# Two hybrid decoder layers on one core: first query tile's items one projection later, its causal mask in the bias table, and the norms' constant on VectorE

## Chip, cores and metric

The kernel runs on one core of one Trainium2 chip. The metric is the time of one execution on the device, in microseconds. Before the change the median of three runs was 1549.06 us (1547.16 to 1550.01).

## The reference

Two decoder layers run over 512 tokens of width 1024. Each layer has a token mixer, a cross attention into 256 memory tokens and a SwiGLU feed-forward network, and behind each of the three stands a layer norm over the residual:

```python
x = layer_norm(ALPHA * x + mixer(x), ln_g[i, 0], ln_b[i, 0])
x = layer_norm(ALPHA * x + cross_attention(x, mem), ln_g[i, 1], ln_b[i, 1])
x = layer_norm(ALPHA * x + swiglu_ffn(x), ln_g[i, 2], ln_b[i, 2])
# layer_norm: (x - mean) * rsqrt(var + 1e-5) * g + b
```

Layer 0 mixes with latent attention (MLA, 16 heads), whose two compressed inputs pass an RMS norm first. Layer 1 mixes with a sparse attention (DSA, 16 heads in 4 groups). A small indexer gives a score to each pair of query and key; for each query the 128 best keys among the earlier ones are kept; the attention logits of the kept keys get a bias, which depends on the distance between query and key and on the head, and all other keys count for nothing:

```python
score = where(causal, sum_h(w_idx * relu(q_idx @ k_idx.T)), -inf)
sel = top_k(score, 128)
logits = q @ k[sel].T * 64 ** -0.5 + rel_bias[t5_bucket(pos_q - pos_k[sel])]
out = softmax(where(sel <= q_index, logits, -inf)) @ v[sel]
```

## The kernel before

**Arithmetic.** A matrix product in f32 is done as three products of rounded parts. Each operand is split into a rounded value (an ACT cast, L98) and the rest (a subtraction, L100, on VectorE (DVE) or GpSimd (POOL)), and TensorE (PE) runs high times high, high times low and low times high (L121 to L123, `mm3`). One projection of 512 tokens onto 128 columns is 24 matmuls of 128x512.

**Stages.** The program has no loop on the device; the Python loops write everything out. Layer 0 is the MLA mixer with its RMS norms (`rms_t`, L508 to L522, eight of them, two for each of four token tiles), then its output projection with the layer norm, the cross attention with its own, and FFN 0 with its own. Then comes layer 1 in the same manner, with the DSA mixer, and the last norm writes the result. The order of each engine's instructions is set by a scheduler from the program's text; the waits between engines are semaphores.

**Layer norm.** `Norm.stat` (L298) takes statistics of a half row of a token tile (L300). `Norm.finish` (L302) joins them (L304) and calls `rstd_of` (L268): on POOL a multiply-add with the constant (L270) and a power of -0.5 (L272). Then, for each half, DVE subtracts the mean and multiplies by the gain (L323), and multiplies by the result of the power and adds the offset (L325); PE transposes the tile (L329) and the transposed tile is split. The last norm of the kernel (L307 to L320) has another form: the two subtractions (L309), then a first piece on DVE (L314), a second one on ACT and POOL (L317, L318), and the write to the output (L319). `LASTS` (L285) sets where these pieces are cut: at column 512, and at 704 in the last token tile. `out_proj` (L345) calls the norm. Its last part runs over the four token tiles; in the last one of the kernel the product is done in two column halves (`TAIL`), each with residual (L341) and statistics, and `finish` of the tile before stands ahead of the first residual (L378). `rms_t` uses `rstd_of` too: an ACT square with a sum, the constant and the power on POOL, then DVE's product with the result (L514).

**DSA mixer.** The value projection, the indexer's projections and its scores come first (L912 to L950). For query tiles 1 to 3 the scores lie in `masks[qt]`, 256, 384 and 512 columns wide. `topk` (L959) does one round: MAX8 (L964) finds the eight largest of a row, MATCH_REPLACE8 (L965) strikes them out. Sixteen rounds make 128 keys, and behind the last one a TENSOR_SCALAR (L969) turns the struck-out places into a mask of 0 and -BIG (2 to the 100th). The 48 rounds of the three tiles are handed out: two ahead of each of two key projections, and five (`NTK`) ahead of each of eight query projections (L1087 to L1101) until none is left. The mask of query tile 0 is plain causality and is written at the start: a POOL memset and select into `mk0f`, and a DVE cast (L956).

Each query projection gives two heads. `stack_q_pool` (L902) splits them: three ACT copies and two POOL subtractions (L907, L908), so that the two parts lie stacked and the scores need two matmuls instead of three. An item is a query tile with a group of four heads, 16 in all, and has three words: `s` (scores, `dsa_scores`, L1003), `t` (transposes, `dsa_t`, L1017) and `p` (times the values, `dsa_pv`, L1034). For each head, `s` runs a product of the identity and the mask (L1011), which puts the mask into the PSUM bank, and two products of Q and K (L1012, L1013); then DVE adds the bias and finds the row's extreme (L410, in `Softmax.exp`) and ACT does the exponential (L416). The table `steps` (L1079) says which words stand behind which query projection, and what follows the loop is written out (L1103 on):

```python
steps = {1: "s0", 2: "t0", 3: "s1 p0", 4: "t1", 5: "s2 p1", 6: "t2", 7: "s3 p2"}
```

Items 0 to 3 are query tile 0. Item 3 needs heads 12 to 15, that is, projections 6 and 7; item 0 needs projections 0 and 1.

**Bias table.** `bias_table` (L246), written ahead of all that and running far earlier, makes the row of biases by distance with a product of the 16 heads' table and a 0/1 matrix `onehot` of 640 (`GW`) columns, in two column blocks, 0 to 512 and 512 to 640. The last 128 columns stand for keys behind the query. The table is spread over a DRAM scratch, from which each item reads its window. `general_bias` (L181) is a branch that runs only where the positions aren't consecutive.

## Time and profile before

| | |
|---|---|
| runs, median (range) | 1549.06 us (1547.16 to 1550.01) |
| the profiled execution | 1549.22 us |
| its span, first to last instruction | 1547.4 us |
| mean granted clock of PE | 0.998 |
| PE busy | 1509.4 us, 98% |
| DVE busy | 997.8 us, 64% |
| ACT busy | 649.9 us, 42% |
| POOL busy | 321.6 us, 21% |
| DRAM read and written | 161.20 and 9.47 MB |

In a row of the timeline the columns are the start in us, the duration in us, the engine, the line, the operation, output and inputs with their sizes, how many instructions the row holds, and in brackets the idle time of the engine just before with the instruction that ended it. In a row of groups the count is followed by the busy time in us and the mean of one in ns, and then by the idle time before them. In a row of waits the idle time of the first engine is followed by how often it occurred and the longest one. In the table of stretches each engine has its busy time and the number of its instructions; the granted clock, the share of the DMA engines and the transfer rate follow. PEld is the loading of weights into PE, which overlaps the matmuls. An engine's idle time costs only where the engine, or someone who waits for it, sets the end.

### The profile page before, as it was taken

The numbers are of one execution on the slowest core, as the hardware profiler recorded it, in microseconds if no ns is written. First come the engines' busy times: TensorE is split into PE (matmuls) and PEld (weight loads), VectorE is DVE, ScalarE is ACT, GpSimd is POOL, SyncE is SP. The second block draws the span as 40 slices with busy tenths as digits, with TensorE's granted clock in tenths as the row PEclk, the third lists the DMA queues.
The fourth block names the chain that finished last, engine by engine and source line by source line (L and its number), as shares of the span: only waits on it lengthen the run. The fifth ranks groups of instructions, "written<-read, shape, count | busy, mean of one in ns | idle before, by whom it ended". The sixth has DMA issues, their size and how long they took to land.

```text
span 1547.4 us, 20800 instructions
## 1 busy us (share of the span) xinstructions
PE 1509.4 (98%) x7940; PEld 1287.3 (83%) x7940; DVE 997.8 (64%) x1709; ACT 649.9 (42%) x1150; POOL 321.6 (21%) x332
## 2 busy tenths in 40 slices
PE   9999999999999999999999899999999999999997
PEld 8788888988888888888887688898988888888886
DVE  6887868454746565654668989675548465656545
ACT  4677743343233333332246568334432333333230
POOL 1322001000132331400124553010002323324003
PEclk9999999999999999999999999999999999999999
DMA  6234424322323232223242147333323232322221
GB/s 221 71 102 116 138 82 133 126 83 95 125 94 109 77 118 92 96 95 109 83 143 96 35 140 255 109 109 110 107 89 132 73 118 88 106 96 93 96 95 55
DMA packets 51320, 166.79 MB, mean 108 GB/s; under 512 B 5300, under 2 KB 11748, under 8 KB 49172
## 3 DMA queue, kind: packets, MB, share of 16 engines
q1 hardware_dynamic: 50788, 164.41, 31.6%
q8 instruction: 62, 1.02, 0.3%
q10 hardware_dynamic: 432, 1.05, 0.2%
q14 instruction: 38, 0.31, 0.1%
HBM read 161.20 MB, written 9.47 MB: 110 GB/s over the span
## 4 chain that ended last, share of the span: by engine, by line
PE 83%; DVE 7%; ACT 3%; POOL 3%; issue 2%; DMA 2%; POOLq 0%; ACTq 0%; DVEq 0%; SPq 0%
PE ps L121 26%; PE ps L123 26%; PE ps L122 26%; DVE t L100 2%; ACT wh L98 1%; DVE wl L100 1%; ACT t L98 1%; PE ps L1028 1%; ACT t L416 1%; PE ps L329 1%; POOL sm L272 1%; DVE t L325 1%; DMA raw<-in_xa_q_dram 1%; POOL sm L270 1%; PE ps L624 1%
## 5 line engine op out<-in xcount | busy, mean ns | idle before, releaser
L121 PE MATMUL ps<-t,wh 128*128 128x512 f32 (+1 forms) x1264 | 459.7, 364 | 3.4 <-DVE t L100 3.4
L122 PE MATMUL ps<-t,wh 128*128 128x512 f32 (+1 forms) x1264 | 458.2, 363 | 1.6 <-DVE t L100 1.6
L123 PE MATMUL ps<-t,wl 128*128 128x512 f32 (+1 forms) x1264 | 458.2, 362 | 0.0
L98 ACT CAST wh<-raw 128x1024 fp32r<-128x1024 f32 (+2 forms) x218 | 227.3, 1044 | 456.3 <-PE ps L122 173.6
L100 DVE TENSOR_TENSOR wl<-raw,wh 128x1024 fp32r<-128x1024 f32 (+2 forms) x197 | 253.8, 1290 | 226.5 <-ACT wh L98 224.8
L121 PE MATMUL ps<-wh,t 128*128 128x512 f32 (+2 forms) x838 | 305.1, 364 | 2.8 <-DVE t L100 1.5
L123 PE MATMUL ps<-wh,t 128*128 128x512 f32 (+2 forms) x838 | 303.1, 362 | 0.0
L122 PE MATMUL ps<-wl,t 128*128 128x512 f32 (+2 forms) x838 | 302.5, 361 | 0.0
L121 PEld LDWEIGHTS ps<-t,wh 128*128 128x128 f32 x1264 | 238.6, 189 | 41.4 <-DVE t L100 5.5
L122 PEld LDWEIGHTS ps<-t,wh 128*128 128x128 f32 x1264 | 238.7, 189 | 38.0 <-DVE t L100 2.0
L123 PEld LDWEIGHTS ps<-t,wl 128*128 128x128 f32 x1264 | 238.6, 189 | 37.1
L121 PEld LDWEIGHTS ps<-wh,t 128*128 128x128 f32 x838 | 159.2, 190 | 26.4 <-DVE t L100 1.7
L123 PEld LDWEIGHTS ps<-wh,t 128*128 128x128 f32 x838 | 159.0, 190 | 23.9 <-DVE t L100 0.3
L122 PEld LDWEIGHTS ps<-wl,t 128*128 128x128 f32 x838 | 159.2, 190 | 23.0
L98 ACT CAST t<-ps 128x512 fp32r<-128x512 f32 (+2 forms) x249 | 122.7, 526 | 132.0 <-PE ps L329 87.4
L270 POOL TENSOR_SCALAR sm<-sm 128x1 f32<-128x1 f32 x32 | 18.9, 590 | 675.7 <-DVE sm L304 634.7
L100 DVE TENSOR_TENSOR t<-ps,t 128x512 fp32r<-128x512 f32 (+2 forms) x249 | 144.1, 606 | 21.6 <-ACT t L98 20.7
L98 ACT CAST wh<-t 128x1024 fp32r<-128x1024 f32 x56 | 58.9, 1052 | 141.6 <-PE ps L122 123.6
L100 DVE TENSOR_TENSOR wl<-t,wh 128x1024 fp32r<-128x1024 f32 x56 | 71.2, 1272 | 64.9 <-ACT wh L98 63.1
L843 DVE TENSOR_TENSOR t<-ps,t 128x512 f32<-128x512 f32 x44 | 30.4, 692 | 120.4 <-PE ps L123 120.4
L100 DVE TENSOR_TENSOR t<-t,t 128x512 fp32r<-128x512 f32 (+2 forms) x113 | 83.9, 746 | 23.6 <-ACT t L98 21.4
L98 ACT CAST t<-t 128x512 fp32r<-128x512 f32 (+2 forms) x113 | 64.4, 574 | 57.9 <-POOL t L777 33.6
(177 smaller groups left out, 1684.1 us busy)
## 6 DMA issues: line engine op xcount, KB each, us to landing
raw<-in_ffn_in_dram SPq DMA_DIRECT2D x88, 512.0 KB, 3.2
t<-in_ffn_dg_dram SPq DMA_DIRECT2D x16, 1024.0 KB, 5.1
raw<-in_xa_k_dram SPq DMA_DIRECT2D x16, 512.0 KB, 3.3
raw<-in_xa_v_dram SPq DMA_DIRECT2D x16, 512.0 KB, 3.7
raw<-in_xa_q_dram SPq DMA_DIRECT2D x16, 512.0 KB, 3.7
raw<-in_xa_o_dram SPq DMA_DIRECT2D x16, 512.0 KB, 3.3
raw<-in_ffn_dl_dram SPq DMA_DIRECT2D x12, 512.0 KB, 3.2
scr<-vscr SPq DMA_DIRECT2D x16, 319.5 KB, 4.2
```

Source lines behind the costliest of these rows:

```text
L98: nc.scalar.copy(h, src)
L100: (eng or nc.vector).tensor_tensor(l, src, h.bitcast(F32), op=ALU.subtract)
L121: nc.tensor.matmul(ps, st[0], mv[0], start=start, stop=False, skip_group_check=more)
L122: nc.tensor.matmul(ps, st[0], mv[1], start=False, stop=False, skip_group_check=more)
L123: nc.tensor.matmul(ps, st[1], mv[0], start=False, stop=stop, skip_group_check=more)
L270: nc.gpsimd.tensor_scalar(a, var, scale, eps, op0=ALU.mult, op1=ALU.add)
L272: nc.gpsimd.tensor_tensor(b, a, mhalf, op=ALU.pow)
L325: nc.vector.scalar_tensor_tensor(x_of(tt)[:, sl], x_of(tt)[:, sl], rs, self.gb[:, 1, sl], op0=ALU.mult, op1=ALU.add)
L329: nc.tensor.transpose(pt[:, k], x_of(tt)[:, 512 * n + P * k:512 * n + P * k + P], ident)
L416: nc.scalar.activation(Sx, src, AF.Exp, bias=nb, scale=scale, accum_out=self.sm[:, i:i + 1])
L624: nc.tensor.transpose(pt[:, P * qt:P * qt + P], Ss[qt][:, P * kb:P * kb + P], ident)
L843: nc.vector.tensor_tensor(sg, pu, sg, op=ALU.mult)
```

## The change

Four things change. The words of items 0 to 3 in `steps` each move one projection later, and s3 and p2 stand directly behind the loop. The mask of query tile 0 goes: `mk0f`, its cast and its entry in `masks` are gone, the product L1011 is only run for tiles 1 to 3, and the last 128 columns of the bias table hold -BIG in place of a bias (a POOL memset and a DMA; the second column block of the product with `onehot` is gone). The branch for other positions gets a select in the diagonal block instead. In `rstd_of` the constant is added on DVE instead of POOL; the power stays on POOL. In the last norm the last tile is cut at 768 instead of 704, and `finish` of the tile before stands behind the first half's residual and statistics instead of ahead of them.

```diff
--- before.py
+++ after.py
@@ -239,6 +239,9 @@
                             if b:
                                 g.tensor_tensor(acc[c], acc[c], tmp, op=ALU.add)
                     for c in range(4):
+                        if kb == qt:
+                            g.affine_select(out=acc[c], in_=acc[c], pattern=[[0, 4], [-1, P]], compare_op=ALU.is_ge,
+                                            fill=-BIG, base=0, channel_multiplier=1)
                         g.dma_start(scr[1 + qt, 4 * c:4 * c + 4, :, c0 + P * kb:c0 + P * kb + P].rearrange("h p k -> p h k"),
                                     acc[c])
         yield
@@ -247,17 +250,16 @@
 
         relb = t2()
         nc.sync.dma_start(relb[0:32, 0:16], A["rel_bias"])
-        cols = ((0, 512), (512, GW))
-        ohs = [t2() for _ in cols]
-        for oh, (lo, hi) in zip(ohs, cols):
-            nc.sync.dma_start(oh[0:32, 0:hi - lo], A["onehot"][:, lo:hi])
+        oh = t2()
+        nc.sync.dma_start(oh[0:32], A["onehot"][:, 0:S])
         yield
-        for oh, (lo, hi) in zip(ohs, cols):
-            pb = bank("a")
-            nc.tensor.matmul(pb[0:16, 0:hi - lo], relb[0:32, 0:16], oh[0:32, 0:hi - lo], start=True, stop=True)
-            vb = t2()
-            nc.scalar.mul(vb[0:16, 0:hi - lo], pb[0:16, 0:hi - lo], 8.0)
-            nc.sync.dma_start(vscr[:, lo:hi], vb[0:16, 0:hi - lo])
+        pb = bank("a")
+        nc.tensor.matmul(pb[0:16], relb[0:32, 0:16], oh[0:32], start=True, stop=True)
+        vb, vn = t2(), t2(F32, (P, GW - S))
+        nc.scalar.mul(vb[0:16], pb[0:16], 8.0)
+        nc.sync.dma_start(vscr[:, 0:S], vb[0:16])
+        nc.gpsimd.memset(vn[0:16], -BIG)
+        nc.sync.dma_start(vscr[:, S:GW], vn[0:16])
         yield
 
     def bias_rows(h):
@@ -267,7 +269,7 @@
 
     def rstd_of(var, scale, eps):
         a = small()
-        nc.gpsimd.tensor_scalar(a, var, scale, eps, op0=ALU.mult, op1=ALU.add)
+        nc.vector.tensor_scalar(a, var, scale, eps, op0=ALU.mult, op1=ALU.add)
         b = small()
         nc.gpsimd.tensor_tensor(b, a, mhalf, op=ALU.pow)
         return b
@@ -282,7 +284,7 @@
         nc.sync.dma_start(gb[:, 1], A["ln_b"][i, j:j + 1].broadcast_to((P, D)))
         return gb
 
-    LASTS = (((0, 512), (512, 1024)), ((0, 704), (704, 1024)))
+    LASTS = (((0, 512), (512, 1024)), ((0, 768), (768, 1024)))
     TAIL = ((0, 256), (256, 512))
 
     class Norm:
@@ -374,10 +376,13 @@
                             sh, sl = src(k)
                             wh, wl = ws[k // 2]
                             mm3(p1[:, c0:c1], (sh[:, ts_], sl[:, ts_]), (wh[:, k % 2, c0:c1], wl[:, k % 2, c0:c1]), k == 0, k == nk - 1)
-                        if tt and c0 == 0:
+                        early = len(parts) > 1
+                        if tt and c0 == 0 and not early:
                             norm.finish(tt - 1)
                         residual(p1, tt, n, first, c0, c1)
                         norm.stat(tt, n, c0, c1)
+                        if c0 == 0 and early:
+                            norm.finish(tt - 1)
                 norm.finish(NT - 1)
 
     HALVES = ((0, 256), (256, 512))
@@ -948,13 +953,7 @@
             if j == 3:
                 nc.gpsimd.affine_select(out=acc[:, n - P:n], in_=acc[:, n - P:n], pattern=[[-1, P]],
                                         compare_op=ALU.is_ge, fill=-1e30, base=0, channel_multiplier=1)
-    mk0f = t2()
-    nc.gpsimd.memset(mk0f[:, 0:256], 0.0)
-    nc.gpsimd.affine_select(out=mk0f[:, 0:256], in_=mk0f[:, 0:256], pattern=[[-1, 256]],
-                            compare_op=ALU.is_ge, fill=-BIG, base=0, channel_multiplier=1)
     MK = t8()
-    nc.vector.tensor_copy(MK[:, 0, 0:256], mk0f[:, 0:256])
-    masks[0] = MK[:, 0]
 
     def topk(qt, its):
         n = P * (qt + 1)
@@ -1008,8 +1007,9 @@
         sx = Softmax([bt[:, i, 0:n] for i in range(4)])
         for i in range(4):
             ps = bank("b")
-            nc.tensor.matmul(ps[:, :N], identr, masks[qt][:, :N], start=True, stop=False)
-            nc.tensor.matmul(ps[:, :N], Q[4 * g + i][:, ts_], KA[g][:, :N], start=False, stop=False)
+            if qt:
+                nc.tensor.matmul(ps[:, :N], identr, masks[qt][:, :N], start=True, stop=False)
+            nc.tensor.matmul(ps[:, :N], Q[4 * g + i][:, ts_], KA[g][:, :N], start=qt == 0, stop=False)
             nc.tensor.matmul(ps[:, :N], Q[4 * g + i][:, ts_], KB[g][:, :N], start=False, stop=True)
             sx.exp(i, ps[:, :n], 0.125, bt[:, i, 0:n])
         return sx
@@ -1076,7 +1076,7 @@
         PT[i] = dsa_t(*items[i], Ss.pop(i))
 
 
-    steps = {1: "s0", 2: "t0", 3: "s1 p0", 4: "t1", 5: "s2 p1", 6: "t2", 7: "s3 p2"}
+    steps = {2: "s0", 3: "t0", 4: "s1 p0", 5: "t1", 6: "s2 p1", 7: "t2"}
 
     def run(word):
         kind, i = word[0], int(word[1:])
@@ -1100,6 +1100,8 @@
         for word in steps.get(j, "").split():
             run(word)
 
+    run_s(3)
+    run("p2")
     run_s(4)
     run_t(3)
     for i in range(3, 16):
```

What this does to the order of the engines' instructions is shown at three places. Line numbers of the changed kernel differ: L410 becomes L415, L964 and L965 become L963 and L964, L969 becomes L968; in the norm L300 becomes L302, L304 L306, L309 L311, L314 L316, L323 L325, L325 L327 and L341 L343.

The first place is PE at the end of the loop over the query projections. `ps_11520` is the bank of projection 7 before, `ps_11532` of the same projection in the changed kernel; `t_1677` and `t_1678` before are the split Q operands of projection 6, and so are `t_1660` and `t_1661` in the changed kernel; `t_1686` there belongs to projection 7. Before:

```order
L123 MATMUL ps_11520<-t_1388_10064,wl_11517 128x512
L1011 MATMUL ps_11555<-t_1536_10860,identr 128x256
L1012 MATMUL ps_11555<-t_1550_10945,t_1677_11477 128x256
L1013 MATMUL ps_11555<-t_1550_10945,t_1677_11477 128x256
L1011 MATMUL ps_11561<-t_1536_10860,identr 128x256
L1012 MATMUL ps_11561<-t_1550_10945,t_1678_11478 128x256
L1013 MATMUL ps_11561<-t_1550_10945,t_1678_11478 128x256
L1011 MATMUL ps_11567<-t_1536_10860,identr 128x256
L1011 MATMUL ps_11573<-t_1536_10860,identr 128x256
L1045 MATMUL ps_11583<-t_1683_11494,t_1449_10402 128x512
```

The changed kernel:

```order
L123 MATMUL ps_11532<-t_1386_10108,wl_11529 128x512
L1026 MATMUL ps_11569<-ident,t_1571_11101 128x128 x4
L1012 MATMUL ps_11581<-t_1547_10983,t_1660_11461 128x256
L1013 MATMUL ps_11581<-t_1547_10983,t_1660_11461 128x256
L1012 MATMUL ps_11586<-t_1547_10983,t_1661_11462 128x256
L1013 MATMUL ps_11586<-t_1547_10983,t_1661_11462 128x256
L1012 MATMUL ps_11591<-t_1547_10983,t_1686_11557 128x256
L1013 MATMUL ps_11591<-t_1547_10983,t_1686_11557 128x256
L104 MATMUL ps_11569<-t_1692_11574,identn 128x512
```

The transposes of t2 (L1026, with L104 as their split on PE) now stand behind the last projection, where they stood behind projection 6 before. The scores of s3 (L1012, L1013) follow and have lost their mask products (L1011). Where p2 (L1045) stood between the first two and the last two heads of s3, three heads and more now stand ahead of it.

The second place is DVE there: the last rounds for query tile 3, whose scores are `t_1462` before and `t_1460` in the changed kernel, and the L410 (L415) of item s3, whose output tile is `t_1598` before and `t_1590` in the changed kernel. Before:

```order
L964 MAX m_1783_11850<-t_1462_10553 128x8
L965 MATCH_REPLACE t_1462_10553<-m_1783_11850,t_1462_10553 128x512
L410 ISA t_1598_11160,sm_11553<-ps_11555,t_1598_11160 128x128
L410 ISA sm_11553 128x1
L410 ISA t_1598_11160,sm_11553<-ps_11561,t_1598_11160 128x128
L410 ISA sm_11553 128x1
L964 MAX m_1803_11921<-t_1462_10553 128x8
L965 MATCH_REPLACE t_1462_10553<-m_1803_11921,t_1462_10553 128x512
```

The changed kernel:

```order
L963 MAX m_1740_11730<-t_1460_10597 128x8
L964 MATCH_REPLACE t_1460_10597<-m_1740_11730,t_1460_10597 128x512
L963 MAX m_1760_11801<-t_1460_10597 128x8
L415 ISA t_1590_11180,sm_11579<-ps_11581,t_1590_11180 128x128
L415 ISA sm_11579 128x1
L415 ISA t_1590_11180,sm_11579<-ps_11586,t_1590_11180 128x128
L415 ISA sm_11579 128x1
L964 MATCH_REPLACE t_1460_10597<-m_1760_11801,t_1460_10597 128x512
```

Before, the last round, that of `m_1803`, stands between the second and the third L410 of s3, and 47 rounds stand ahead. In the changed kernel the round of `m_1760`, the 46th, is begun ahead of s3's first L415 and ended behind the second; those of `m_1780` and `m_1800` come behind all four, the latter directly ahead of the mask's TENSOR_SCALAR (L968).

The third place is DVE at the end of the kernel, from the third token tile's aggregate on. `t_1990` before and `t_1987` in the changed kernel hold the third and the fourth token tile of x; `t_2693` and `t_2690` are gain and offset; `sm_17074` and `sm_17098` are the third tile's mean and variance, `sm_17110` and `sm_17132` the fourth's. Before:

```order
L304 BN_AGGR sm_17074<-sm_16943 128x2
L309 SCALAR_TENSOR_TENSOR t_1990_12593<-t_1990_12593,sm_17074,t_2693_16839 128x512 x2
L314 SCALAR_TENSOR_TENSOR t_1990_12593<-t_1990_12593,sm_17078,t_2693_16839 128x512
L341 TENSOR_TENSOR t_1990_12593<-t_1990_12593,ps_17055 128x256
L300 BN_STATS sm_16946<-t_1990_12593 128x6
L341 TENSOR_TENSOR t_1990_12593<-t_1990_12593,ps_17089 128x256
L300 BN_STATS sm_16946<-t_1990_12593 128x6
L304 BN_AGGR sm_17110<-sm_16946 128x2
L309 SCALAR_TENSOR_TENSOR t_1990_12593<-t_1990_12593,sm_17110,t_2693_16839 128x704
L309 SCALAR_TENSOR_TENSOR t_1990_12593<-t_1990_12593,sm_17110,t_2693_16839 128x320
L314 SCALAR_TENSOR_TENSOR t_1990_12593<-t_1990_12593,sm_17114,t_2693_16839 128x704
```

The changed kernel:

```order
L306 BN_AGGR sm_17098<-sm_16965 128x2
L272 TENSOR_SCALAR sm_17100<-sm_17098 128x1
L311 SCALAR_TENSOR_TENSOR t_1987_12615<-t_1987_12615,sm_17098,t_2690_16861 128x512
L343 TENSOR_TENSOR t_1987_12615<-t_1987_12615,ps_17077 128x256
L311 SCALAR_TENSOR_TENSOR t_1987_12615<-t_1987_12615,sm_17098,t_2690_16861 128x512
L302 BN_STATS sm_16968<-t_1987_12615 128x6
L316 SCALAR_TENSOR_TENSOR t_1987_12615<-t_1987_12615,sm_17102,t_2690_16861 128x512
L343 TENSOR_TENSOR t_1987_12615<-t_1987_12615,ps_17111 128x256
L302 BN_STATS sm_16968<-t_1987_12615 128x6
L306 BN_AGGR sm_17132<-sm_16968 128x2
L272 TENSOR_SCALAR sm_17134<-sm_17132 128x1
L311 SCALAR_TENSOR_TENSOR t_1987_12615<-t_1987_12615,sm_17132,t_2690_16861 128x768
```

L272 in the changed kernel is the constant. The last tile's first residual (L343 with `ps_17077`) and statistics (L302) now stand within the `finish` of the tile before, not behind it, and the last pieces are 768 and 256 columns wide; on the output queue the piece of 256 columns is written first and that of 768 columns last, where before 704 columns were written first and 320 last.

## Prediction

> **What bounds the kernel now.** I read the page first, then who PE waits for, then a table by stage.
>
> ```profile
> PE 1509.4 (98%) x7940; PEld 1287.3 (83%) x7940; DVE 997.8 (64%) x1709; ACT 649.9 (42%) x1150; POOL 321.6 (21%) x332
> PE ps L1012 <- POOL t L907: 4.8, 5, 1.5
> PE ps L1012 <- POOL t L908: 3.2, 5, 0.7
> ```
>
> PE is busy for 1509.4 of 1547.4 us, so all its idle time is 38 us and a change of order can win only from that. The two rows with POOL are the largest share that the change touches: 4.8 + 3.2 = 8.0 us in ten waits, where the score items of query tile 0 (s0 to s3) want Q operands that POOL is still splitting.
>
> ```profile
> 825.00:850.00 25.00, 23.23 (x105) 18.65 (x104) 23.12 (x65) 17.38 (x29) 13.68 (x12) 1.00 0.33 107
> 850.00:875.00 25.00, 21.29 (x103) 16.70 (x102) 23.50 (x72) 11.73 (x28) 13.84 (x13) 1.00 0.19 62
> 875.00:900.00 25.00, 23.16 (x116) 18.59 (x115) 22.66 (x56) 12.15 (x26) 12.34 (x14) 1.00 0.09 28
> ```
>
> These are the stretches of those waits. The columns are the length, then PE, PEld, DVE, ACT and POOL. The average of DVE over the kernel is 64%, but here it is busy for 23.1, 23.5 and 22.7 of 25 us, about as much as PE. That decides what the lost waits are worth.
>
> **Part 1: the items of query tile 0, one projection later.**
>
> ```profile
> 901.92 0.39 PE L1012 MATMUL ps<-t,t 128*128 128x256 f32 x1 [0.79 <-POOL t L907]
> 903.26 0.38 PE L1012 MATMUL ps<-t,t 128*128 128x256 f32 x1 [0.61 <-POOL t L908]
> 866.03 0.28 PE L1011 MATMUL ps<-t,identr 128*128 128x256 f32 x1
> 866.15 0.28 PE L1012 MATMUL ps<-t,t 128*128 128x256 f32 x1
> ```
>
> For PE alone: s3 needs the last projection, so it stands where it stood and its waits of 0.79 + 0.61 = 1.40 us stay. The other 8.0 - 1.4 = 6.6 us go, since a whole projection now lies between a split and its use. The 16 mask products (L1011) of these items go too. One takes the 0.12 us from 866.03 to 866.15, so 16 x 0.12 = 1.9 us. PE alone would gain 8.5 us.
>
> Now DVE, which works in order through the top-k rounds (MAX8 and MATCH_REPLACE8) and the scores' L410:
>
> ```profile
> 828.64 0.43 DVE L964 MAX8 m<-t 128x8 f32<-128x256 f32 x1 [0.18 <-POOL t L949]
> 849.96 2.30 DVE L969 TENSOR_SCALAR t<-t 128x256 fp32r<-128x256 f32 x1
> 874.43 0.37 DVE L969 TENSOR_SCALAR t<-t 128x384 fp32r<-128x384 f32 x1
> 904.02 0.84 DVE L1053 TENSOR_TENSOR t<-ps,t 64x256 f32<-64x256 f32 x2
> L410 DVE CUSTOM_DVE_ANT_0 t<-ps,t 128x128 f32<-128x128 f32 x32 | 8.9, 283 | 4.0 <-PE ps L1013 3.8
> L956 DVE CAST t<-t 128x256 fp32r<-128x256 f32 x1 | 0.4, 377 | 0.0
> ```
>
> All 48 rounds and the four items' L410 lie between 828.64 and 904.02, 75.4 us. In them DVE idled for PE only in front of the 128x128 L410: 3.8 us. The rounds are not made fewer. In the new order 46 of them still start ahead of s3's first L410 (47 before), and the other two come ahead of masks[3]. So even if PE is early by 8.5 us, DVE can finish this work earlier only by its own idle time, 3.8 us, and the dropped cast L956, 0.3 to 0.4. I take 4.1 us. PE then waits for DVE, through the exponentials at t2 and through the four PSUM banks at s4.
>
> What can move this is the cast of a mask (L969). It took 2.30 us for 256 columns and 0.37 for 384:
>
> ```profile
> 849.72 2.39 POOL L100 TENSOR_TENSOR wl<-raw,wh 128x1024 fp32r<-128x1024 f32 x1
> ```
>
> The long one began 0.24 us behind this POOL split and ended 0.15 us behind it. [...] Two casts lie inside the stretch, one long and one short, so meeting none wins 1.9 us more and meeting both loses 1.9. Part 1: -4.1, from -2.2 to -6.0.
>
> **Part 2: the constant of a norm on DVE.** POOL's L270 goes, DVE gets a 128x1 TENSOR_SCALAR, whose price is in the trace:
>
> ```profile
> L415 DVE TENSOR_SCALAR sm<-sm 128x1 f32<-128x1 f32 x32 | 4.6, 147 | 0.2
> 762.32 1.41 DVE L325 SCALAR_TENSOR_TENSOR t<-t,sm,t 128x512 f32<-128x512 f32 x2 [0.44 <-POOL sm L272]
> 763.12 1.32 PE L329 MATMUL ps<-ident,t 128*128 128x128 f32 x8 [0.31 <-DVE t L325]
> 775.07 0.66 PE L329 MATMUL ps<-ident,t 128*128 128x128 f32 x4 [0.38 <-DVE t L325]
> ```
>
> Behind FFN 0 the order is aggregate, two L323, L325, and L325 idles 0.44 us for POOL's power. POOL's two small operations outlast the two L323; the power alone does not. So the idle 0.44 becomes the added 0.11 (0.147, its end overlapped). PE's waits there are 0.31 for the first tile and 0.38 for the third, with one alike between them: 3 x 0.3 = 0.9 us gone.
>
> In four other norms (behind the MLA and DSA mixers and both cross attentions) it goes the other way for the last tile:
>
> ```profile
> 257.80 0.55 POOL L272 TENSOR_TENSOR sm<-sm,mhalf 128x1 f32<-128x1 f32 x1
> 258.11 1.23 DVE L100 TENSOR_TENSOR wl<-raw,wh 128x1024 fp32r<-128x1024 f32 x1 [0.68 <-ACT wh L98]
> 260.58 1.41 DVE L325 SCALAR_TENSOR_TENSOR t<-t,sm,t 128x512 f32<-128x512 f32 x2
> ```
>
> Here POOL had the power done at 258.35, under a weight split that DVE ran and waited 0.68 for. In the new order that split stands ahead of the TENSOR_SCALAR, so POOL starts only when DVE is through with it (259.3). What such a late power costs:
>
> ```profile
> 425.43 1.41 DVE L323 SCALAR_TENSOR_TENSOR t<-t,sm,t 128x512 f32<-128x512 f32 x2
> 425.64 0.94 POOL L272 TENSOR_TENSOR sm<-sm,mhalf 128x1 f32<-128x1 f32 x1
> ```
>
> A power issued 0.2 us into the first L323 ended 0.44 us behind that one's end (426.14), within the second. So it is ready before the pair ends and the loss is the added 0.11 to 0.2 us: 4 x 0.15 = +0.6.
>
> The eight RMS norms of the MLA mixer:
>
> ```profile
> 38.10 1.15 POOL L272 TENSOR_TENSOR sm<-sm,mhalf 128x1 f32<-128x1 f32 x1
> 53.90 0.74 DVE L514 SCALAR_TENSOR_TENSOR t<-ps,sm,t 128x512 f32<-128x512 f32 x1
> 56.06 2.05 DVE L560 TENSOR_TENSOR t<-t,t 64x512 f32<-64x512 f32 x1
> 59.08 0.69 DVE L561 TENSOR_TENSOR t<-t,t 64x512 f32<-64x512 f32 x1
> 59.10 0.50 PE L122 MATMUL ps<-t,wh 128*128 128x512 f32 x1 [1.62 <-DVE t L100]
> ```
>
> For the last tile the TENSOR_SCALAR stands directly ahead of L514, so DVE stands still there for a power, 0.55 to 1.15 us. But L560 behind it lasts 2.05 us against 0.69 for L561 of the same shape, and started later it meets less of what holds it up. I take 0, from -0.6 to +0.6. Part 2: -0.9 + 0.6 + 0 = -0.3, from -1.2 to +1.0.
>
> **Part 3: the end.**
>
> ```profile
> 1529.57 0.39 PE L123 MATMUL ps<-wh,t 128*128 128x512 f32 x1
> 1533.65 0.39 PE L123 MATMUL ps<-wh,t 128*128 128x512 f32 x1
> 1530.14 0.68 DVE L341 TENSOR_TENSOR t<-t,ps 128x512 f32<-128x512 f32 x1
> 1534.35 0.68 DVE L341 TENSOR_TENSOR t<-t,ps 128x512 f32<-128x512 f32 x1
> 1540.25 0.24 DVE L304 BATCH_NORM_AGGREGATE sm<-sm 128x2 f32<-128x18 f32 x1
> 1542.38 0.95 DVE L314 SCALAR_TENSOR_TENSOR t<-t,sm,t 128x704 f32<-128x704 f32 x1 [0.44 <-POOL sm L272]
> 1543.02 1.03 POOL L318 TENSOR_TENSOR t<-t,t 128x320 f32<-128x320 f32 x1 [0.67 <-ACT t L317]
> out_dram<-t SPq DMA_DIRECT2D x1, 352.0 KB, 2.3
> out_dram<-t SPq DMA_DIRECT2D x1, 160.0 KB, 2.0
> ```
>
> PE ends a tile each 4.08 us (1533.65 - 1529.57). DVE needs 4.21 for one now (1534.35 - 1530.14), and 4.21 - 0.44 + 0.11 = 3.88 then, so PE sets the pace up to the last matmul. The half tile's residual and statistics now come ahead of the previous tile's L314, and the last aggregate moves from 1540.25 to about 1539.5. From there DVE's L314 waits now 2.13 us, then 0.24 + 0.11 + 1.41 = 1.76. That is 0.75 + 0.37 = 1.1 us for DVE and about as much for POOL's piece. Less comes out: the write of 768 columns (384 KB, some 2.4 us) now stands behind that of POOL's 256 columns on SP, while today the last write is the small one, 2.0 us. So 1.1 - 0.4 = 0.7, less a little for the queue: -0.6, from -0.2 to -1.2.
>
> The bias table loses a small product and an evacuation and gains a memset of a row block, all in front of work that PE does meanwhile: 0. The fallback branch with the added selects isn't taken, as its cost shows nowhere in this trace.
>
> **The sum.** -4.1 - 0.3 - 0.6 = -5.0 us against the profiled execution, 1549.22 us (span 1547.4 and 1.8 around it); the median of the runs is 1549.06. That gives 1544.2 us. Its own range is from 1541 to 1547. A difference of 0.2%, 3.1 us, is about what a measurement of this kernel can tell from none.
>
> **Rivals.**
> - *PE sets the pace in the stretch after all*, because the rounds that remain behind s3 find gaps. For it: DVE has pauses from 905 on. Against it: 46 rounds ahead of s3. Then 8.5 instead of 4.1: 1539.8 us. Chance 0.14.
> - *The gain is given back behind the last projection.* t2, s3 and p2 now stand there with no projection between them; before, a projection covered t2. If PE pays the exponentials and s3's POOL waits one after another, some 3 us of the 4.1 are lost: 1547.3 us. For it: s3 waited 1.40 us even with p2 and s4 in front. Against it: DVE isn't through with the rounds then anyway. Chance 0.12.
> - *The power waits for both L323 or both L309.* [...] From the rows: the four last tiles lose 4 x 0.7, FFN 0's norm gains nothing, the end nothing: -4.1 + 2.8 = -1.3, 1547.9 us. Against it: the power at 425.64, through within the second. Chance 0.06.
> - *Slower: the RMS norms.* If DVE stands still for each of the eight powers as long as the longest took (1.15 and 0.11 of hand-over) and nothing absorbs it, 8 x 1.26 = 10.1 us are added: 1554.3 us. It is slower from 8.1 us of stall on (5.0 + 3.1). Against it: PE is busy throughout until 51 us, and DVE has pauses there. Chance 0.05.
> - *The waits don't go*, since POOL is late by more than a projection: about 1549. Chance 0.03.
>
> My forecast has 0.60, of which 0.04 is within 0.2%. Faster by over 0.2%: 0.56 + 0.14 = 0.70. Within: 0.04 + 0.12 + 0.06 + 0.03 = 0.25. Slower: 0.05. The range from 1540.0 to 1547.6 leaves out the slow case, the locked power and half of the first rival: 0.18.
>
> **What would show it.** Right: the rows L1012 <- POOL shrink to s3's alone; DVE's idle time ahead of the 128x128 L410 is near 0; PE has new waits for ACT's exponential or DVE between 880 and 900; L325's idle time for POOL is gone in FFN 0's norm; the last three tiles of the end follow each other at 4.1 us. Wrong: PE without new waits up to 905 (the first rival), or L1012 waits as long as now.

## The result, and the profile after

The changed kernel takes 1538.99 us (median of six runs, 1537.31 to 1541.90), the kernel before 1549.38 us (six runs): a ratio of 0.9934, 95% interval 0.9923 to 0.9945. The change wins 10.4 us, twice the 5.0 of the forecast, and the time lies 1.0 us below the range. Its profiled execution took 1539.14 us, its span 1537.3.

The page's first part and the waits of PE in the changed kernel, in the columns of before, and last a row of before:

```profile
PE 1507.6 (98%) x7922; PEld 1288.3 (84%) x7922; DVE 994.0 (65%) x1740; ACT 651.0 (42%) x1149; POOL 304.7 (20%) x299
PE ps L1012 <- POOL t L912: 3.2, 2, 2.7
PE ps L1012 <- POOL t L913: 1.4, 2, 0.8
PE ps L331 <- DVE t L327: 1.2, 1, 1.2
PE ps L329 <- DVE t L325: 5.3, 7, 1.3
```

The ten waits for POOL's Q splits have become four, 4.6 us in place of 8.0, but one of them is 2.7 us long. The last two rows are PE's waits for the product with the power (L325, L327 now): before, there were seven of 5.3 us together, and one is left. My argument had priced only the three in FFN 0.

Where the time came from is read by setting PE's own rows of the two traces side by side. Here is one matmul behind the DSA mixer's items, and one in the last product, each first in before, then in the changed kernel:

```profile
984.42 0.39 PE L123 MATMUL ps<-wh,t 128*128 128x512 f32 x1
1529.35 0.39 PE L122 MATMUL ps<-wl,t 128*128 128x512 f32 x1
```

```profile
977.56 0.39 PE L123 MATMUL ps<-wh,t 128*128 128x512 f32 x1
1519.66 0.39 PE L122 MATMUL ps<-wl,t 128*128 128x512 f32 x1
```

PE is 6.86 us ahead at the first and 9.69 at the second. Taken ahead of and behind each stage, the offset splits the gain (a minus is faster):

| stage | offset of PE ahead of it, behind it | measured, us | forecast, us |
|---|---|---|---|
| up to the end of the MLA mixer (RMS norms, bias table) | 0, -0.10 | -0.1 | 0 |
| norm behind the MLA mixer | -0.10, -1.36 | -1.3 | +0.15 |
| norm behind cross attention 0 | -1.34, -0.69 | +0.65 | +0.15 |
| norm behind FFN 0 | -0.69, -2.06 | -1.4 | -0.9 |
| DSA mixer | -2.06, -6.86 | -4.8 | -4.1 |
| norm behind the DSA mixer | -6.86, -8.26 | -1.4 | +0.15 |
| norm behind cross attention 1 | -8.30, -9.68 | -1.4 | +0.15 |
| the end (1549.22 and 1539.14 us) | -9.68, -10.08 | -0.4 | -0.6 |

The DSA mixer and the end came out near their terms. Three of the four norms that were to lose 0.15 won 1.3 to 1.4 each.

**In the DSA mixer**, the stretches of the forecast and then the end of the loop in steps of 2 us (length, PE, PEld, DVE, ACT, POOL, granted clock, DMA):

```profile
825.00:850.00 25.00, 25.00 (x113) 20.75 (x112) 23.37 (x68) 16.75 (x27) 13.73 (x9) 1.00 0.38 116
850.00:875.00 25.00, 23.38 (x117) 19.26 (x116) 24.00 (x75) 16.24 (x35) 13.76 (x13) 1.00 0.17 54
875.00:900.00 25.00, 21.39 (x107) 18.25 (x106) 21.66 (x68) 13.75 (x40) 14.62 (x21) 0.86 0.20 64
```

```profile
890.00:892.00 2.00, 0.46 (x3) 0.41 (x3) 1.97 (x8) 0.77 (x4) 1.84 (x3) 1.00 0.33 110
892.00:894.00 2.00, 1.44 (x6) 0.93 (x5) 0.64 (x6) 1.09 (x5) 0.84 (x1) 0.52 0.00 0
896.00:898.00 2.00, 2.00 (x12) 2.00 (x11) 1.96 (x8) 1.36 (x6) 0.00 (x0) 0.50 0.00 0
898.00:900.00 2.00, 2.00 (x15) 2.00 (x15) 1.18 (x7) 1.78 (x6) 1.43 (x5) 0.77 0.01 4
```

PE has no gap in the first stretch, 1.6 us of gaps in the second (1.3 of them two waits of s0 for POOL that stayed, 0.47 and 0.84), and a hole at 890. Directly behind the hole the clock that PE is granted falls to half, until 898.9. The rows of ACT, POOL and PE there, and those of DVE:

```profile
888.01 0.58 ACT L910 CAST t<-ps 64x512 fp32r<-64x512 f32 x1
888.21 0.29 POOL L1061 CAST t<-t 128x128 fp32r<-128x128 f32 x1 [3.87 <-DVE t L1057]
889.35 0.45 POOL L1062 TENSOR_TENSOR t<-t,t 128x128 fp32r<-128x128 f32 x1
889.75 0.40 POOL L426 COPY t<-sm 128x256 f32<-128x256 f32 x1
890.23 1.26 POOL L912 TENSOR_TENSOR t<-t,t 64x512 fp32r<-64x512 f32 x1
881.10 0.40 PE L1045 MATMUL ps<-t,t 128*128 128x512 f32 x1
891.54 0.38 PE L1012 MATMUL ps<-t,t 128*128 128x256 f32 x1 [2.75 <-POOL t L912]
893.49 0.63 PE L1045 MATMUL ps<-t,t 128*128 128x512 f32 x1
893.73 0.29 DVE L415 CUSTOM_DVE_ANT_0 t<-ps,t 128x128 f32<-128x128 f32 x1 [1.34 <-PE ps L1013]
895.22 0.42 DVE L415 CUSTOM_DVE_ANT_0 t<-ps,t 128x256 f32<-128x256 f32 x1 [0.59 <-PE ps L1013]
```

The split of the last projection (L912) stands on POOL behind the output split of p1 (L1061, L1062) and a copy of t2 (L426). Its input was ready at 888.59, when ACT's L910 ended, and it began at 890.23. PE waits 2.75 us for it; then a matmul of 512 columns (L1045) takes 0.63 us, where it took 0.40 at 881.10. DVE waits for PE here (1.34 and 0.59), not PE for DVE: the prediction had it the other way round. DVE still has a hand in it: POOL had waited 3.87 us for DVE's L1057 before it could begin the output split that stood in the way.

**In a norm** (here behind the MLA mixer), DVE's rows of the last tile, and the wait that is left, behind cross attention 0:

```profile
249.55 1.41 DVE L327 SCALAR_TENSOR_TENSOR t<-t,sm,t 128x512 f32<-128x512 f32 x2
256.66 0.21 DVE L306 BATCH_NORM_AGGREGATE sm<-sm 128x2 f32<-128x12 f32 x1
256.89 1.22 DVE L100 TENSOR_TENSOR wl<-raw,wh 128x1024 fp32r<-128x1024 f32 x1
258.04 0.15 DVE L272 TENSOR_SCALAR sm<-sm 128x1 f32<-128x1 f32 x1
423.66 1.23 DVE L100 TENSOR_TENSOR wl<-raw,wh 128x1024 fp32r<-128x1024 f32 x1 [1.19 <-ACT wh L98]
427.09 0.63 PE L331 MATMUL ps<-ident,t 128*128 128x128 f32 x4 [1.21 <-DVE t L327]
```

The weight's split ahead of the constant waited 0.68 us for ACT before and doesn't wait now. Its place ahead of the constant is as forecast; that it had to wait as long as before was my assumption. In cross attention 0 the opposite happened: no wait before, 1.19 now.

### The profile page after: what moved, and what is told of

It reads as the page before. It is cut to its first block, busy times and chain, and to the rows that moved or that the text cites. A ratio compares the mean times of both kernels' runs of the same rounds, so it can differ in the third digit from the quotient of the medians.

```text
span 1537.3 us, 20760 instructions
## 1 busy us (share of the span) xinstructions
PE 1507.6 (98%) x7922; PEld 1288.3 (84%) x7922; DVE 994.0 (65%) x1740; ACT 651.0 (42%) x1149; POOL 304.7 (20%) x299
## 3 DMA queue, kind: packets, MB, share of 16 engines
q8 instruction: 62, 1.02, 0.3%
q10 hardware_dynamic: 432, 1.05, 0.2%
## 4 chain that ended last, share of the span: by engine, by line
PE 85%; DVE 6%; ACT 3%; issue 2%; POOL 2%; DMA 1%; POOLq 0%; SPq 0%; ACTq 0%; DVEq 0%
PE ps L121 26%; PE ps L123 26%; PE ps L122 26%; DVE t L100 2%; PE ps L331 1%; ACT t L421 1%; ACT t L98 1%; ACT wh L98 1%; DVE wl L100 1%; POOL wl L100 1%; PE ps L629 1%; DMA t<-in_xT_dram 0%; PE ps L1028 0%; PE ps L1026 0%; POOL sm L274 0%
## 5 line engine op out<-in xcount | busy, mean ns | idle before, releaser
L274 POOL TENSOR_TENSOR sm<-sm,mhalf 128x1 f32<-128x1 f32 x32 | 29.4, 918 | 691.9 <-DVE sm L272 691.9
```

The costliest lines, as they stand in the source:

```text
L274: nc.gpsimd.tensor_tensor(b, a, mhalf, op=ALU.pow)
```

## The experiments

Theory A: the constant on DVE is worth 4.8 us in the norms. Theory B: the last tiles won because weights happened to land early. Theory P: in the DSA mixer PE sets the pace up to the last projection, and there POOL and a halved clock take some of the gain back. Theory D: DVE sets the pace, as predicted. All runs are compared with runs of the kernel before on the same chip; the ratio for the changed kernel is 0.9934.

**const_pool**, the changed kernel with

```diff
-        nc.vector.tensor_scalar(a, var, scale, eps, op0=ALU.mult, op1=ALU.add)
+        nc.gpsimd.tensor_scalar(a, var, scale, eps, op0=ALU.mult, op1=ALU.add)
```

> The changed kernel with the constant of the norms back on POOL, nothing else undone. Theory A: the norms were the mis-sized step; the constant on DVE takes the 0.44 us idle time ahead of the product with the power, DVE frees a weight buffer earlier, and the split of a weight ahead of the last tile is no longer late. By the offset of PE between the two traces the norms gave 1.25 + 1.37 + 1.45 + 1.35 - 0.6 = 4.8 us, so 1539.0 + 4.8 = 1543.8, with seven waits of PE for DVE's second product, 5 us together. Theory B: the last tiles gained because weight transfers happened to land early, which has nothing to do with the constant; only the 0.9 us of FFN 0's norm are lost: 1539.9, and few waits come back.

Measured: 1544.67 us, ratio 0.9965 (0.9952 to 0.9979); 5.7 us more than the changed kernel by the medians, 4.8 by the ratios. PE's rows that waited for the product with the power, of the four last tiles:

```profile
260.00 0.63 PE L331 MATMUL ps<-ident,t 128*128 128x128 f32 x4 [1.23 <-DVE t L327]
426.60 0.63 PE L331 MATMUL ps<-ident,t 128*128 128x128 f32 x4 [0.98 <-DVE t L327]
1021.39 0.63 PE L331 MATMUL ps<-ident,t 128*128 128x128 f32 x4 [0.44 <-DVE t L327]
1189.67 0.67 PE L331 MATMUL ps<-ident,t 128*128 128x128 f32 x4 [2.68 <-DVE t L327]
```

Seven waits of 6.3 us are back, those of FFN 0 among them. But the waits of the last tiles run from 0.44 to 2.68, which the constant alone doesn't explain. Behind the last of them the clock was halved for 3.41 us, and by its offset PE lost 4.3 us in that one norm.

**norm_only**, the kernel before with

```diff
-        nc.gpsimd.tensor_scalar(a, var, scale, eps, op0=ALU.mult, op1=ALU.add)
+        nc.vector.tensor_scalar(a, var, scale, eps, op0=ALU.mult, op1=ALU.add)
```

> The kernel before with the constant of the norms on DVE and nothing else. Theory A (the idle time ahead of the product with the power, and through it the weight's split): 4.8 us less than before, about 1544.5, and the waits of PE for DVE's second product fall from 5.3 us to 1 or 2. Theory B (transfers landed early by chance): 0.9 us less, 1548.5, with waits in three or four last tiles.

Measured: 1545.88 us, ratio 0.9973 (0.9963 to 0.9982), 4.2 us less than before (2.8 to 5.7); the waits for the product with the power are 1.9 us. Both runs speak for A, but the weights' landings differ from kernel to kernel, so B stays open.

**What delays a weight.** The split ahead of the last tile waits for ACT's cast, and the cast for a weight's transfer. The transfer is issued when DVE has split an earlier weight and so freed its buffer. Here are that split, the first issue on SP's queue and the cast, behind the MLA mixer, in before and then in the changed kernel:

```profile
251.44 1.23 DVE L100 TENSOR_TENSOR wl<-raw,wh 128x1024 fp32r<-128x1024 f32 x1
252.69 5.02 SPq L111 DMA_DIRECT2D raw<-in_xa_q_dram  x3
257.03 1.05 ACT L98 CAST wh<-raw 128x1024 fp32r<-128x1024 f32 x1 [3.66 <-DMA raw<-in_xa_q_dram]
```

```profile
250.88 1.22 DVE L100 TENSOR_TENSOR wl<-raw,wh 128x1024 fp32r<-128x1024 f32 x1
252.12 5.02 SPq L111 DMA_DIRECT2D raw<-in_xa_q_dram  x3
255.81 1.06 ACT L98 CAST wh<-raw 128x1024 fp32r<-128x1024 f32 x1 [2.52 <-DMA raw<-in_xa_q_dram]
```

Directly ahead of the first of these rows stands the third tile's product with the power, in before with an idle time:

```profile
250.11 1.42 DVE L325 SCALAR_TENSOR_TENSOR t<-t,sm,t 128x512 f32<-128x512 f32 x2 [0.44 <-POOL sm L272]
```

In the changed kernel DVE no longer idles there (249.55 above), so the split and the issue are 0.57 us earlier, 0.1 of it from the stages ahead. But from issue to cast it took 4.34 us before and 3.69 now, and in cross attention 0 it took 3.66 before and 4.85 now (issues at 419.54 and 417.73). The trace's DMA packets show what else is under way: single packets of 16 KB in the queue that the profile calls q8 instruction.

```profile
q8 instruction: 62, 1.02, 0.3%
```

That is 62 packets with 1.02 MB together. Between two of them PE begins 253 matmuls and weight loads on average in the changed kernel, from 186 to 313, while DVE's count runs from 10 to 85 and the time from 14.0 to 31.3 us. I took them for PE's instructions, which is an estimate from these counts. In cross attention 0 of the changed kernel one began at 420.08, 2.35 us behind the weight's issue, and took 1.16 us. In the 13 traces of this case there are 52 such weights (four norms each):

| packet begins behind the issue | cases | issue to cast, us |
|---|---|---|
| 0.05 to 1.14 us | 17 | 3.66 to 4.61 |
| 1.5 to 2.54 us | 6 | 4.73 to 5.80 |
| 2.57 to 4.93 us | 29 | 3.14 to 3.75, one 5.75 |

**warm2 and warm2_const_pool** move the packets against PE's work, in the changed kernel and in const_pool:

```diff
-WARM = 8
+WARM = 2
```

> The changed kernel with 2 instead of 8 warm-up matmuls at the start, which takes 24 instructions (12 matmuls and 12 weight loads) out of PE's queue and so moves each 16 KB packet of instructions that is fetched for PE about 2.7 us later against PE's work. Theory F: such a packet, when it is fetched 0 to 1.2 or 2.3 to 2.6 us behind the issue of the weight that the last tile of a norm waits for, delays that weight; moved 2.7 us later it lies behind the landing in all four norms, each weight lands 3.2 to 3.7 us behind its issue (4.85 in the norm of layer 0's cross attention now), and PE's wait of 1.21 us there falls to 0.3 or less: 1 us less, but for what the start loses. Theory C: how long a weight takes has other reasons; the 4.85 and the 1.21 stay.

> As the run with 2 warm-up matmuls, and with the constant of the norms back on POOL. Theory F: the packets of instructions lie behind the landings here too, so the weights land after 3.2 to 3.7 us (4.34, 4.05, 3.47 and 5.80 now), and what is left between the two kernels is what the constant on POOL costs by itself: 0.3 us in three tiles of FFN 0, about 0.5 in each of the four last tiles, 0.6 to 1.1 at the end: some 3.5 us in place of 5.7. Theory C: the landings stay where they are, with a wait of 2.7 us in the norm of layer 1's cross attention, and the difference stays near 5.7.

Measured: 1537.40 us, ratio 0.9924 (0.9908 to 0.9940), and 1540.79 us, ratio 0.9947 (0.9931 to 0.9962). The packets now begin 2.6 us or more behind all eight issues (against PE they moved less than the 2.7 us expected, 0.9 to 2.3 in the first of the two and 0.0 to 2.7 in the second), and all eight weights take 3.1 to 3.4 us. The cast in cross attention 0 of warm2, and the four last tiles of warm2_const_pool:

```profile
420.22 1.05 ACT L98 CAST wh<-raw 128x1024 fp32r<-128x1024 f32 x1 [2.10 <-DMA raw<-in_ffn_in_dram]
421.65 1.17 DVE L100 TENSOR_TENSOR wl<-raw,wh 128x1024 fp32r<-128x1024 f32 x1
```

```profile
259.12 0.63 PE L331 MATMUL ps<-ident,t 128*128 128x128 f32 x4 [0.42 <-DVE t L327]
425.18 0.63 PE L331 MATMUL ps<-ident,t 128*128 128x128 f32 x4 [0.44 <-DVE t L327]
1019.31 0.63 PE L331 MATMUL ps<-ident,t 128*128 128x128 f32 x4 [0.44 <-DVE t L327]
1185.39 0.63 PE L331 MATMUL ps<-ident,t 128*128 128x128 f32 x4 [0.44 <-DVE t L327]
```

In warm2 no wait for the product with the power is left. With the landings equal, the constant is worth 1540.79 - 1537.40 = 3.4 us. By the ratios it is 3.6. The two profiled executions differ by 3.7, and PE's offset says where: 2.2 in the four last tiles (0.53 to 0.55 each), 1.4 in FFN 0, 0.7 at the end, 0.2 in the DSA mixer, less 0.8 in the RMS norms. The offset is larger than the idle time in the rows (0.42 to 0.44 in a last tile), because a matmul's row reaches past the place where the next one can start: 0.28 us long at 866.03 in before, with the next start 0.12 behind it. So A holds for 3.4 to 3.6 of the 4.8 to 5.7 us between const_pool and the changed kernel, and the rest is B's, but it goes with something that the traces show: whether a packet begins within 2.54 us of the weight's issue, as in the table. How a packet would hold a weight up isn't shown.

**items_mask and items_move**: the kernel before with the whole of the items' part of the change; and with the moves alone, the mask products kept:

```diff
-    steps = {1: "s0", 2: "t0", 3: "s1 p0", 4: "t1", 5: "s2 p1", 6: "t2", 7: "s3 p2"}
+    steps = {2: "s0", 3: "t0", 4: "s1 p0", 5: "t1", 6: "s2 p1", 7: "t2"}
...
+    run_s(3)
+    run("p2")
     run_s(4)
```

> The kernel before with the items of query tile 0 one projection later and their mask in the bias table, norms and tail as before. Theory P (PE sets the pace up to the last projection; behind it s3 waits for POOL and the granted clock is halved): the eight waits of s0 to s2 go, 6.6 us, and 1.9 us of mask products; s3's waits for POOL grow from 1.4 to about 3.3 and some 7 us at half clock cost about 3: 4.8 less, 1544.5. Theory D (DVE sets the pace, as predicted): 4.1 less, 1545.2, with no idle time of DVE up to the end of s3 and without need of the half clock; where the clock isn't halved, the time is the same.

> The kernel before with the items of query tile 0 one projection later, but with the mask products of query tile 0 kept. Theory P (PE sets the pace): the waits of s0 to s2 for POOL go as with the mask in the bias table, and the 16 mask products stay, 0.12 us each: 1.9 us more than the run with both, 5.2 less than before. Theory D (DVE sets the pace): only the cast of the mask is more work for DVE, 0.4 us: within 0.5 of the run with both.

Measured: items_mask 1543.03 us, ratio 0.9954 (0.9941 to 0.9968); items_move 1544.18 us, ratio 0.9966 (0.9953 to 0.9978). The items' part wins 7.1 us (5.0 to 9.1). Its profiled execution, whose time of 1547.39 is the longest of the five, gives 4.6 us for the DSA mixer by PE's offset (-0.2 ahead of it, -4.8 behind), and lost 3.0 again in the norm behind cross attention 1, where a weight came 5.75 us behind its issue and the clock was halved for 3.41 us; by their times, the other executions didn't lose that. By time the two runs don't settle P against D. items_move is 1.2 us behind items_mask by the medians and 1.9 by the ratios, where P had 1.9 and D 0.4, and the intervals overlap. They also differ in more than the mask products: in items_move PE waits 1.70 us for DVE's L1053 at 877.42, which it doesn't in items_mask. By PE's offset between the two, items_mask is 0.6 us behind ahead of the DSA mixer, 1.8 ahead at 897, and 0.4 ahead at 900, because its clock was halved for 6.83 us there and that of items_move for 3.41.

**mask_only**: the kernel before with the mask in the bias table alone, that is, the change's hunks on `general_bias`, `bias_table`, `mk0f` and `dsa_scores`, at its core

```diff
-            nc.tensor.matmul(ps[:, :N], identr, masks[qt][:, :N], start=True, stop=False)
+            if qt:
+                nc.tensor.matmul(ps[:, :N], identr, masks[qt][:, :N], start=True, stop=False)
```

> The kernel before with the mask of query tile 0 in the bias table and the items left where they were. By the sum of the prediction the 16 mask products are 1.9 us of PE's time, so 1.9 less than before. Against it: in each of s0 to s3 the products run while the last two heads wait for POOL, so without them PE only comes to the same wait earlier, and the waits for POOL grow from 8.0 us by about as much: the same time as before within 0.5.

Measured: 1550.21 us, ratio 1.0010 (1.0000 to 1.0020). No gain. PE's waits for POOL in it:

```profile
PE ps L1009 <- POOL t L909: 5.6, 5, 1.7
PE ps L1009 <- POOL t L910: 3.3, 5, 0.8
```

They grew from 8.0 to 8.9 us: PE comes to the same waits earlier. That is half of the 1.9; in this execution the clock was also halved for 3.41 us at 853.77, which cost PE about 1.5. With the items moved, the products are worth 1.2 to 1.9 us by the two runs above, which isn't clear of noise.

**s4_first**: the changed kernel with

```diff
+    run_s(4)
     run_s(3)
     run("p2")
-    run_s(4)
```

> The changed kernel with the scores of item 4 ahead of those of item 3, so that PE has twelve matmuls of ready operands, 1.5 us and more, while POOL splits the last Q. Theory P: of s3's 3.3 us of waiting 1.5 to 2 go, the pause stays too short for the clock to be halved (about 3 us more): 3 to 5 us less than the changed kernel, 1534 to 1536. Theory D: DVE sets the pace and has the same work; the time stays at 1539 within 1, and PE waits elsewhere.

Measured: 1536.49 us, ratio 0.9913 (0.9899 to 0.9926), 3.3 us less than the changed kernel by the ratios, 2.5 by the medians, at or under the low end of P's 3 to 5. PE in it at the place of the wait, and the clock:

```profile
891.37 0.36 PE L1012 MATMUL ps<-t,t 128*128 128x256 f32 x1 [1.02 <-DVE sm L415]
```

```profile
892.00:894.00 2.00, 2.00 (x14) 1.63 (x13) 1.91 (x12) 2.00 (x8) 0.76 (x1) 1.00 0.00 0
894.00:896.00 2.00, 2.00 (x20) 2.00 (x18) 1.93 (x5) 1.94 (x9) 0.00 (x0) 1.00 0.00 0
```

The wait of 2.75 us is down to 1.02 and the clock stays full. D had the time stay within 1 us. Here, with POOL's wait filled, PE's wait is for DVE. By the starts of PE's matmuls in the DSA mixer, 3.8 us of waits for POOL and 2.9 of half clock go, and 4.0 come back, most of them in waits for DVE and ACT: these are the next limit, close behind.

**rounds_later**: the changed kernel with

```diff
-    NTK, NTI = 5, 1
+    NTK, NTI = 4, 2
```

> The changed kernel with four instead of five top-k rounds ahead of each query projection and two instead of one behind each item, so that two or three rounds fewer of 1.5 us each stand ahead of s3 on DVE. Theory D (DVE sets the pace there): up to 3 us less, 1536. Theory P (PE sets it, and at s3 POOL does): the wait of 2.7 us for POOL and the half clock stay, and the time is 1539 within 1.

Measured: 1538.17 us, ratio 0.9924 (0.9911 to 0.9937), 1.5 below the changed kernel by the ratios and 0.8 by the medians; the intervals overlap. The edit moved nothing. In both traces PE, DVE, ACT and POOL do the same operations in the same order, and 46 rounds are begun ahead of s3's first L415 in both. So this run is the changed kernel once more, with the same wait of 2.74 us at s3, and says nothing for P or against D; whether fewer rounds ahead of L1057 would shorten the wait stays untested. It shows the price of the clock instead: halved for 3.41 us here and for 6.83 there, and by PE's offset this execution gained 1.2 us between 896 and 900.

**old_tail**: the changed kernel with the end of before:

```diff
-    LASTS = (((0, 512), (512, 1024)), ((0, 768), (768, 1024)))
+    LASTS = (((0, 512), (512, 1024)), ((0, 704), (704, 1024)))
...
-                        if tt and c0 == 0 and not early:
+                        if tt and c0 == 0:
                             norm.finish(tt - 1)
...
-                        if c0 == 0 and early:
-                            norm.finish(tt - 1)
```

> The changed kernel with the end of the kernel before (cut at 704, the norm of the third tile ahead of the last tile's first half). By the prediction it is 0.6 slower than the changed kernel, as the new order wins that much. The traces of the other runs speak against it: with the constant on DVE and the old order the last write was issued 4.87 us behind the last matmul, with the new order 5.16, and the last piece to be written is larger: 0.3 to 0.7 faster than the changed kernel.

Measured: 1537.63 us, ratio 0.9920 (0.9906 to 0.9934), 1.4 below the changed kernel by the medians and 2.2 by the ratios, with overlapping intervals, so it is not slower. The difference is too small for the runs, but not for the traces: from the start of the last matmul to the end of the span there are 9.36 us before, 8.22 in norm_only and 8.29 here (old end, constant on DVE), 8.93 in the changed kernel and 9.66 in const_pool (new end, constant on POOL). (Two more kernels with the old end and the constant on POOL have 9.61, mask_only, and 10.26, items_mask, whose last write took 2.87 us to land instead of 2.04.) The last writes of the changed kernel (size, us to landing) stand in the order of the forecast, the large one issued last:

```profile
out_dram<-t SPq DMA_DIRECT2D x1, 384.0 KB, 2.4
out_dram<-t SPq DMA_DIRECT2D x1, 128.0 KB, 1.8
```

The constant wins 1.1 us with the old end and 0.7 with the new one, and the new end loses 0.6: the last write is issued 5.16 us behind the start of the last matmul instead of 4.87, and lands after 2.39 instead of 2.05. The cut at 768 and the new order came together, so their shares aren't shown.

**combo**: the edits of s4_first, old_tail and warm2 together, which is what the runs point to.

> The changed kernel with what the runs so far point to: item 4's scores ahead of item 3's (3.2 us less), the old end (0.6 less), 2 warm-up matmuls (about 1.5 less). If they add up, 5 us less than the changed kernel: 1534. If the packets of instructions fall into a weight's landing again, since the order of PE is another one, up to 2 us of it are lost.

Measured: 1534.19 us, ratio 0.9902 (0.9887 to 0.9916): 4.8 us less than the changed kernel and 15.2 less than before. The parts add up; its clock was full from 12.1 us to 1527.6.

## Why the prediction was wrong

It had the direction, and a range whose low end is 1.0 us too high. (The range also left out the rival at 1549, so 0.21 and not 0.18 lay outside it.) The step that failed is in part 2: "In four other norms [...] it goes the other way for the last tile", "4 x 0.15 = +0.6". Measured there: -1.3 + 0.65 - 1.4 - 1.4 = -3.4 us, 4.0 below the term, of the 5.1 us by which the profiled execution lies below the forecast.

- *Four norms.* I followed the instructions of the last tile alone and left the row of its wait (0.68) as it stood. That wait ends with a weight that lands, and the weight's buffer is freed by DVE three tiles into the norm, which the constant makes earlier by dropping an idle time of 0.44 that I had counted in FFN 0 only. By the pair of runs with fewer warm-up matmuls this wins 0.53 to 0.55 us of PE's time in each of the four. The rest, both the larger gains and the loss in cross attention 0, goes with where the packets of q8 instruction fell: from issue to cast the four weights took 4.34, 3.66, 4.41 and 4.38 us before and 3.69, 4.85, 3.21 and 3.43 now. These differences, less 0.54 each, are -1.2, +0.65, -1.7 and -1.5, against the measured -1.3, +0.65, -1.4 and -1.4. No row that I quoted could have told that; a wider range for a transfer's landing (3.1 to 5.8 us here) could. The waits of before had a warning: 5.3 us for the product with the power in seven places, of which I priced the three in FFN 0. The other four, 1.23 + 0.58 + 1.32 + 1.26 = 4.4 us, stand in these four norms.
- *FFN 0's norm:* right in its mechanism, -1.4 for -0.9. I took the idle times of the rows (0.96 in the three waits), which are less than what a wait costs PE.
- *The RMS norms:* -0.1 for 0, within the bounds. The stall of the slow rival didn't come. Where the constant alone differs, it cost PE 0.6 us there between const_pool and the changed kernel, 0.8 between the two runs with fewer warm-up matmuls, and nothing between before and norm_only.
- *The locked power*, the rival in which the power waits for both products: no run shows its 0.7 us for each of four last tiles. In the last tile behind the MLA mixer the power was issued at 258.26 and took 0.99, through before the second product (259.42), and no wait of DVE for the power ahead of a second product is left in any norm. That rival fell.
- *The DSA mixer:* -4.8 for -4.1, within the bounds, but for another reason. I let DVE set the pace. The first rival was right about PE up to 887 (no new waits), and s4_first speaks for PE and POOL. It gave 8.5, not 4.8, and what is missing shows when the starts of PE's matmuls are held against their usual distance (227 ns for 512 columns, 120 for 256). The waits for POOL cost 10.7 us before and 5.6 now: two of s0's stayed (0.47 and 0.84), and s3's grew from 1.40 to 3.31. The 6.83 us at half clock cost 2.9, and other waits shrank by 0.7. With the 1.9 of the mask products that is 5.1 + 1.9 + 0.7 - 2.9 = 4.8. The second rival had the place and another price: I had asked what covers t2, s3 and p2, and not what stands on POOL ahead of the last split.
- *The casts of the masks* were both short (0.44 and 0.36 us): no weight split ran on POOL when they began, as one end of the bounds had it. What such a split costs a cast no run shows beyond the one long cast of before (2.30 us).
- *The end:* -0.4 for -0.6, but as the sum of -1.1 for the constant and +0.6 for the new order. I had let the order win and the write cost 0.4; the new end costs more at the last write than DVE saves.

## What to carry to other kernels

Follow a wait back to what ends it before you price what stands behind it: a split that waits for a cast that waits for a transfer moves with the instruction that frees the transfer's buffer, which may be three tiles away. When work is moved to where nothing covers it, look at each in-order queue that feeds it (here POOL's) for what stands ahead, and fill the pause with work whose operands are ready. Look in the trace whether an edit moved anything before its time is read: one run here was the changed kernel again. And where a small edit wins several times its own price, equalise what it shifted by accident, as the two runs with fewer warm-up matmuls did, before believing it.

## What the runs showed of the hardware

**The clock behind a pause.** In all eight runs with the 2.7 us wait at s3, PE's clock was halved behind it, for 3.41 or 6.83 us. In before, waits of 1.05, 0.72, 1.46 and 0.62 us within 8 us had no such effect, nor had 1.67 and 0.62 in mask_only; in norm_only and mask_only like ones (1.04 and 0.73; 1.27 and 0.62) were followed by 3.41 us at half clock. In the changed kernel a wait of 2.56 us, which ended at 53.73, had no such effect either, so the length of a wait alone doesn't tell them apart.

From 20 us on, the changes of the clock in a trace lie whole multiples of 3.413 us apart: in the changed kernel 880.64, 6.83 and 634.88 us, which are 258, 2 and 186 of them. Divided from a change on into stretches of that length, the 13 traces give 5725 stretches at full clock. The 14 in which PE's rows leave 51% or more idle (up to 81%) were each followed by half clock; none of the others, with up to 50%, was. Of the 17 stretches at half clock, the three with 16 to 18% of idle time were followed by a second one, which makes 6.83 us, and those with up to 11% by full clock. These are counts of this case; what makes the clock change isn't shown.

In the changed kernel the wait of 2.75 us lies in one stretch, from 888.66 to 892.08, in which PE is busy for 0.67 us, and the clock is halved from 892.08 to 898.90. The wait of 2.56 us lies across two stretches, which leave 36% and 39% idle. The waits of some 1.8 us together in norm_only and mask_only fell into one stretch each.

**Instruction packets and transfers.** In the 52 cases a 16 KB packet of q8 instruction took 0.92 to 1.8 us. A 512 KB weight with a packet 0.05 to 2.54 us behind its issue came 3.66 to 5.80 us behind that issue, the others 3.14 to 3.75, but for one of 5.75. With six warm-up matmuls fewer at the start, in warm2, the weight of cross attention 0 was cast 3.23 us behind its issue (416.99 to 420.22) in place of 4.85, and PE's wait of 1.21 us for the product with the power was gone there.
